# 42 gathered tokens and three products a chunk in a decoder layer's expert mixer

## The chip, the core and the metric

The kernel runs on one core of a Trainium2 chip. Its time is the device time of one launch in microseconds. The kernel before takes 2087.37 us (median of 3 runs, 2080.51 to 2088.08).

## What is computed

One layer over 264 tokens: 256 of a new sequence and 8 samples that continue sequences with a paged cache of 1024 keys and values. Cut to what matters:

```
proj = x @ w_in                                   # 2048 -> rec_x, rec_g, q, k, v (1024 each)
rec  = rg_lru(causal_conv(rec_x)) * gelu(rec_g)   # recurrence over the tokens
att  = rms_norm(diff_attention(rope(q), rope(k), v))   # samples attend to the paged cache
x1   = layer_norm(alpha * x + concat(rec, att) @ w_out)
# expert retrieval: 8 heads, product keys, the best 16 of 128 x 128 experts for a head
e, g = top_16(x1 @ wq, sub_keys), softmax(scores)
out  = sum over k of g * gelu(x1 . u[e_k]) * v[e_k]
y    = layer_norm(alpha * x1 + out)
```

All data is float32, and the tables u and v hold 16384 experts of 2048 numbers each.

## The kernel before

Activations lie with the model's dimension on the 128 partitions, in 16 chunks, and the tokens in the columns. A float32 product is made of fp32r products: each operand is split into a rounded high part (ScalarE, line 97) and a rest (VectorE, line 100), and hi x hi, hi x lo and lo x hi are summed in PSUM. Weights come in halves of 512 KB ("raw", six buffers) on SP's queue.

The program is written in one order for all engines, without a scheduler: what stands first in the code stands first on its engine. In the mixer, generators are advanced one turn at a time between groups of 12 projection products, so a `yield` more or less moves an instruction against the other engines'. The projection `proj` (lines 294 to 296) uses three products of 264 columns for each chunk. `softmax` turns the scores of the 8 samples on the cached keys into weights (`z`, `en`, matrix `C` and the products of line 596), and `values` then multiplies cached value pages. Constants are loaded on ScalarE's queue (`cload`, line 73), results of the mixer are stored on SP's.

The expert mixer treats ND = 232 of the tokens by going through all 128 blocks of 128 experts: `up` (lines 1183 and 1184) makes x1 . u for a block, `act_sum` and `act_gelu` add two halves and apply GeLU, `gate_mult` and `gate_low` multiply by the tokens' gates and split again, `down` (lines 1234 and 1235) multiplies by v, and `add` (line 1242) adds into the residual. `up` and `down` make two products for a chunk: the high weights times the high and the low activations side by side (464 columns), and the low weights times the high activations (232 columns). The two halves of the sum are put together by VectorE. Six of the up blocks are native float32 products. The other NG = 32 tokens get their experts by indirect DMA (`gathered`): 128 rows at a time, 32 tokens by 4 experts, for each table in two halves, and VectorE multiplies them (lines 1386 and 1400); turns of this generator are given out at GRATE a step of the loop. `Norm` is the layer norm, whose sums of squares run on VectorE, ScalarE and GpSimd while the last blocks are multiplied.

Of the kernel before, what the change touches and what calls it, by code (L numbers as in the profile page):

```python
# [18 lines left out]
NC_ = 16  # L19
# [4 lines left out]
NG = 32  # L24
ND = T - NG
REP = 128 // NG
RAWB = 6
# [6 lines left out]
RECB = 4  # L34
# [14 lines left out]
GRATE = 1.5  # L49
# [7 lines left out]
def _build(tc, I, O):  # L57
# [3 lines left out]
    with ctx:  # L61
# [78 lines left out]
        parts0 = pool_in(ctx, "parts0", 2, "right")  # L140
# [9 lines left out]
        own_slots = 2 * [lambda: [parts0.tile([128, 8, 128], F32R, name=k) for k in ("hi", "lo")]]  # L150
# [27 lines left out]
        ident = cload("ident", [128, 128])  # L178
        iota = cload("iota", [128, 128])
# [5 lines left out]
        cosT = cload("cosT", [128, T], pool=sa)  # L185
        sinT = cload("sinT", [128, T], pool=sa)
        blk4 = cload("blk4", [128, 4], pool=sa)
        pti = sa.tile([1, 64], I32, name="pti")
        nc.scalar.dma_start(pti, I["pt"])
        lv = sw.tile([128, 4, 64], F32, name="t", bufs=RECB)  # L190
        nc.scalar.dma_start(lv, bcast(I["lamv"], 128))
        maskn = cload("maskn", [128, 128], pool=sa)
        two = cload("two", [128, 2], pool=sa)
        cp = cload("cp", [128, 128], pool=sa)
        cn = cload("cn", [128, 128], pool=sa)
        own = cload("own", [128, 16], pool=sa)
        subg = cload("subg", [128, 1], pool=sa)
        cw = cload("cw", [128, 8, 4], pool=sa)
        cb = cload("cb", [128, 8], pool=sa)
        ba = cload("ba", [128, 8], pool=sa)  # L200
        bx = cload("bx", [128, 8], pool=sa)
        lam = cload("lam", [128, 8], pool=sa)
        h0 = cload("h0", [128, 8, 8], pool=sa)
        XS = sa.tile([128, 8, 4, 8], F32, name="XS")
        nc.scalar.dma_start(XS[:, :, 0:3, :], I["sconv"])
# [47 lines left out]
        vnat = x0w[:, 2080:2080 + 2048].rearrange("p (k d) -> p k d", k=2)  # L253
# [44 lines left out]
        def qk(g, pa, pb):  # L298
# [23 lines left out]
            else:  # L322
                nc.sync.dma_start(O["kT"][2 * (g - 4)], A)
                nc.sync.dma_start(O["kT"][2 * (g - 4) + 1], B)
# [20 lines left out]
        def vproj(h, pv):  # L345
# [5 lines left out]
            nc.sync.dma_start(O["vT"][h], vT)  # L351
# [12 lines left out]
        def head(hp, qt, h4):  # L364
# [36 lines left out]
            wT = sw.tile([128, 256], F32, name="wT", bufs=3)  # L401
# [64 lines left out]
        def rec(n, px):  # L466
# [4 lines left out]
            nc.sync.dma_start(wg, I["wax"][:, n])  # L471
# [14 lines left out]
            nc.sync.dma_start(O["convp"][:, n], last)  # L486
# [24 lines left out]
            hs = sw.tile([128, T], F32, name="hs")  # L511
# [8 lines left out]
            nc.sync.dma_start(O["hT"][:, n], hs[:, SEQ - 1:T])  # L520
# [40 lines left out]
        def softmax(sps):  # L561


            P = sx[0].tile([128, 2, 512], F32, name="cv", bufs=PAGEB)
            mx = sa.tile([128, 4], F32, name="mx")
            yield
            for a in range(2):
                nc.vector.tensor_reduce(mx[:, a:a + 1], sps[a].rearrange("p j k -> p (j k)"), op=OP.max, axis=AX.X)
            while not all(("qk", g) in done for g in range(8)):
                yield  # L570
# [11 lines left out]
            done.add("scores")  # L582
# [6 lines left out]
            nc.vector.tensor_copy(en, zz[:, 2:3].to_broadcast([128, 2]))  # L589
            yield  # L590
            W = sa.tile([128, NPG, 128], F32, name="Wk")
            for a in range(0, NPG, 4):
                yield from take("misc")
                p = pmisc([128, 4, 128])
                for j in range(4):
                    nc.tensor.matmul(p[:, j, :], P[:, a // 4, j * 128:(j + 1) * 128], C, start=True, stop=True)
                yield
                nc.scalar.copy(W[:, a:a + 4], p)
                give("misc")
# [9 lines left out]
        def values():  # L609
            while "scores" not in done:  # L610
                yield
# [41 lines left out]
            yield from rms(at, 128, 1, sw.tile([128, 1, 128], F32, name="hs"))  # L653
# [65 lines left out]
        nc.gpsimd.memset(QS, 0.0)  # L719
# [7 lines left out]
        for i, j in enumerate(seq):  # L727
# [5 lines left out]
            if i == 17:  # L733
                slots[:] = own_slots
# [25 lines left out]
        nc.sync.dma_start(O["convs"], XS[:, :, 1:4, :])  # L760
# [46 lines left out]
        class Norm:  # L807
# [43 lines left out]
            def squares(self, c):  # L851

                for k in {9: (0, 1, 2), 10: (3, 4, 8), 11: (5, 9), 12: (6, 10), 13: (7, 11, 12), 14: (13, 14), 15: (15,)}.get(c, ()):
                    self.square(k)

            def stats(self, n):

                self.totals()
                mean, rstd = self.mean, self.rstd
                nc.scalar.copy(mean, self.ps)  # L860
                nc.vector.tensor_tensor(rstd, self.ps, self.near, op=OP.subtract)
# [15 lines left out]
            def scale(self, a, n):  # L877
# [38 lines left out]
        x1s = big.tile([128, NC_, 2, T], F32R, name="A")  # L916
# [21 lines left out]
        Es = dram.tile([2, 64, 16], F32, name="Es")  # L938
# [122 lines left out]
        for m in range(2, 16):  # L1061
# [9 lines left out]
            if m < 10:  # L1071

                for c in range(2 * (m - 2), 2 * (m - 2) + 2):
                    nc.scalar.copy(x1s[:, c, 0], x1[:, c, :])
                    nc.vector.tensor_tensor(x1s[:, c, 1], x1[:, c, :], x1s[:, c, 0], op=OP.subtract)
            elif m < 14:
                rows_out(m - 10)
# [10 lines left out]
        def tokens(tt):  # L1088
# [19 lines left out]
            for bk, (a0, n) in enumerate(blocks):  # L1108
# [3 lines left out]
                for t4 in range(0, n, 4):  # L1112
                    t0 = a0 % 128 + t4
                    b = tw[0].tile([128, 4, 128], F32, name="gb", bufs=4)
                    if t4 % 8 == 0:
                        for q in range(4):
                            nc.scalar.activation(b[:, q, :], iota, AF.Abs, bias=tr[3][:, t0 + q:t0 + q + 1])
                        nc.scalar.activation(b, b, AF.Relu, scale=-1.0, bias=1.0)
                    else:
                        nc.vector.tensor_tensor(b, iota[:, None, :].to_broadcast([128, 4, 128]),  # L1120
                                                tr[1][:, t0:t0 + 4, None].to_broadcast([128, 4, 128]), op=OP.is_equal)
                    a = tw[0].tile([128, 4, 128], F32, name="ga", bufs=4)
                    for q in range(4):
# [5 lines left out]
                    def product(a=a, b=b, st=st, t4=t4, n=n, bk=bk):  # L1129
                        p = psum.tile([128, 4, 128], F32, name="acc2")  # L1130
                        for q in range(4):
                            nc.tensor.matmul(p[:, q, :], b[:, q, :], a[:, q, :], start=True, stop=True)  # L1132
                        nc.scalar.copy(st[:, :, t4:t4 + 4], p.rearrange("p t i -> p i t"))
                        if t4 + 4 == n:
# [5 lines left out]
        def gates():  # L1140
# [17 lines left out]
            nc.gpsimd.dma_start(Es[0], ef)  # L1158
            nc.gpsimd.dma_start(Es[1], top.g[:, 0])
# [12 lines left out]
        def up(k, a=0, b=NC_):  # L1172
            w = ups[k]
            if a == 0:
                pu[k] = pmm([128, 2, ND])
            p = pu[k]
            if k < NAT:
                for c in range(a, b):
                    native(p[:, 0], w, c, ND)
                return  # L1180
# [5 lines left out]
        def act_sum(k):  # L1186
            p = pu.pop(k)
            acts[k] = ex.tile([128, ND], F32, name="ac", bufs=RUN - 8)
# [358 lines left out]
```

## Time and profile before

| what | value |
|---|---|
| median of 3 runs | 2087.37 us |
| the profiled execution's own time | 2081.43 us |
| its span | 2079.7 us |
| PE busy | 1996.2 us (96%) |
| DVE busy | 1584.6 us (76%) |
| ACT busy | 973.8 us (47%) |
| POOL busy | 213.6 us (10%) |
| mean granted TensorE clock | 0.988 |
| read from HBM | 499.65 MB |

PE is TensorE's matmuls, PEld its weight loads, which run beside matmuls, DVE VectorE, ACT ScalarE, POOL GpSimd and SP the engine whose queue issues most transfers. The mixer lasts to about 470 us, its norm and the choice of experts to about 825 us, and the loop over the expert blocks to about 2050 us. A wait is shown as idle time of an engine and the instruction that ended it.

### The profile page before, as it was taken

Reading aid. Unit: us, or ns where it says so; the run is one execution under the profiler, and the core shown is the slowest. Engines: PE = TensorE matmul, PEld = TensorE weight load, DVE = VectorE, ACT = ScalarE, POOL = GpSimd, SP = SyncE. Lnnn points to the kernel's source line nnn. Section 1 sums busy time; section 2 is a strip of 40 time slices with the busy share of each in tenths; the row PEclk is TensorE's granted clock in tenths of the full one; section 3 lists DMA queues with packets and bytes.
Section 4 is the critical chain, followed back from the end, with each engine's and each line's share of the span. In section 5 each row is a group of like instructions: output and inputs, shape, how many; then the busy total and the mean of one; then the engine's idle time right before and its main releaser. Section 6 shows DMA issues by size and latency. Waiting matters only on the chain.

```text
span 2079.7 us, 37180 instructions
## 1 busy us (share of the span) xinstructions
PE 1996.2 (96%) x13890; PEld 1829.5 (88%) x13890; DVE 1584.6 (76%) x3231; ACT 973.8 (47%) x1609; POOL 213.6 (10%) x179
## 2 busy tenths in 40 slices
PE   7999789989899999999999999999999999999995
PEld 6888677789788999999999999999999999999994
DVE  5534655775599789668888888888888888878886
ACT  4223554633211798554444444444444444444444
POOL 0000000004000000001111111111222222100011
PEclk9999999999999999999999999999999999999998
DMA  8799489765344567778888888888888888866661
GB/s 283 270 364 326 154 291 318 249 204 166 105 143 135 172 235 253 259 259 292 292 287 304 280 296 300 279 286 275 289 295 277 300 302 280 302 216 219 225 208 51
DMA packets 183622, 522.07 MB, mean 251 GB/s; under 512 B 28858, under 2 KB 61650, under 8 KB 181394
## 3 DMA queue, kind: packets, MB, share of 16 engines
q1 hardware_dynamic: 160400, 451.34, 63.6%
q0 software_dynamic: 18688, 67.41, 9.7%
q8 instruction: 109, 1.79, 0.3%
q10 hardware_dynamic: 4354, 0.96, 0.2%
q14 instruction: 71, 0.58, 0.1%
HBM read 499.65 MB, written 19.97 MB: 250 GB/s over the span
## 4 chain that ended last, share of the span: by engine, by line
PE 77%; DVE 4%; ACT 3%; DMA 2%; issue 1%; POOL 1%; SPq 0%; POOLq 0%; ACTq 0%; DVEq 0%
PE mm L1183 19%; PE acc L1234 18%; PE mm L1184 9%; PE acc L1235 9%; PE mm L920 7%; PE mm L1234 3%; PE mm L1235 1%; PE acc L1132 1%; PE mm L294 1%; PE acc L635 1%; DMA cv<-in_cv 1%; PE mm L295 1%; PE mm L296 1%; DMA raw<-in_uT 1%; ACT hi L97 1%
## 5 line engine op out<-in xcount | busy, mean ns | idle before, releaser
L100 DVE TENSOR_TENSOR lo<-raw,hi 128x1024 fp32r<-128x1024 f32 x326 | 397.4, 1225 | 282.8 <-ACT hi L97 268.9
L1183 PE MATMUL mm<-A,hi 128*128 128x464 f32 x1728 | 568.3, 380 | 0.0
L1234 PE MATMUL acc<-w,xl 128*128 128x464 f32 x1640 | 532.7, 376 | 0.0
L1184 PE MATMUL mm<-A,lo 128*128 128x232 f32 x1728 | 465.8, 270 | 0.7 <-DVE lo L100 0.7
L1235 PE MATMUL acc<-w,xl 128*128 128x232 f32 x1640 | 443.0, 270 | 0.0
L97 ACT CAST hi<-raw 128x1024 fp32r<-128x1024 f32 x326 | 329.4, 1045 | 159.5 <-PE mm L295 70.3
L97 ACT CAST xl<-raw 128x1024 fp32r<-128x1024 f32 x260 | 269.2, 1046 | 220.9 <-issue 193.4
L1183 PEld LDWEIGHTS mm<-A,hi 128*128 128x128 f32 x1728 | 324.6, 188 | 42.1
L100 DVE TENSOR_TENSOR xl<-raw,xl 128x1024 fp32r<-128x1024 f32 x260 | 316.6, 1226 | 31.2 <-ACT xl L97 28.8
L1234 PEld LDWEIGHTS acc<-w,xl 128*128 128x128 f32 x1640 | 307.8, 188 | 35.9
L1184 PEld LDWEIGHTS mm<-A,lo 128*128 128x128 f32 x1728 | 330.6, 191 | 1.0 <-DVE lo L100 1.0
L1235 PEld LDWEIGHTS acc<-w,xl 128*128 128x128 f32 x1640 | 312.7, 191 | 0.0
L1217 ACT CAST w<-ac 128x232 fp32r<-128x232 f32 x128 | 49.5, 387 | 335.4 <-DVE ac L1215 332.6
L1242 DVE TENSOR_TENSOR M<-M,acc 128x232 f32<-128x232 f32 x444 | 166.9, 393 | 29.9 <-PE acc L1235 22.3
L920 PE MATMUL mm<-M,raw 128*128 128x264 f32 (+1 forms) x704 | 156.5, 383 | 7.1 <-ACT M L881 7.1
L920 PEld LDWEIGHTS mm<-M,raw 128*128 128x128 f32 x704 | 134.6, 193 | 25.6 <-ACT M L881 7.5
L294 PE MATMUL mm<-xh,hi 128*128 128x264 f32 x448 | 137.7, 307 | 14.2 <-ACT hi L97 8.3
L296 PE MATMUL mm<-xh,lo 128*128 128x264 f32 x448 | 129.5, 289 | 0.5 <-DVE lo L100 0.5
L295 PE MATMUL mm<-xl,hi 128*128 128x264 f32 x448 | 129.3, 289 | 0.2 <-DVE xl L173 0.2
L1368 POOL DMA_INDIRECT ug<-in_v,eix x64 | 87.8, 1373 | 375.5 <-DVE xrep L1400 305.3
L1368 POOL DMA_INDIRECT ug<-in_u,eix x64 | 79.6, 1244 | 441.0 <-DVE ug L1386 348.5
L294 PEld LDWEIGHTS mm<-xh,hi 128*128 128x128 f32 x448 | 86.6, 193 | 31.2 <-issue 15.5
(357 smaller groups left out, 3114.0 us busy)
## 6 DMA issues: line engine op xcount, KB each, us to landing
raw<-in_uT SPq DMA_DIRECT2D x256, 512.0 KB
raw<-in_vt SPq DMA_DIRECT2D x256, 512.0 KB
raw<-in_w_in SPq DMA_DIRECT2D x74, 512.0 KB
cv<-in_ck SPq DMA_DIRECT2D x64, 512.0 KB
cv<-in_cv SPq DMA_DIRECT2D x64, 512.0 KB
raw<-in_wq SPq DMA_DIRECT2D x32, 512.0 KB
Gd<-stage SPq DMA_DIRECT2D x14, 1024.0 KB
gt<-Gd SPq DMA_DIRECT2D x224, 64.0 KB
```

The lines of the kernel that those rows point to most:

```text
L97: nc.scalar.copy(hi, raw)
L100: (eng or nc.vector).tensor_tensor(lo, raw, hi, op=OP.subtract)
L294: nc.tensor.matmul(p, hi, xh[:, c], start=c == 0, stop=False)
L295: nc.tensor.matmul(p, hi, xl[:, c], start=False, stop=False)
L296: nc.tensor.matmul(p, lo, xh[:, c], start=False, stop=c == NC_ - 1)
L920: nc.tensor.matmul(p, w[c // 8][:, c % 8, :], x1[:, c, :n], start=c == 0, stop=c == NC_ - 1)
L1183: nc.tensor.matmul(p, hi[:, c % 8, :], x1s[:, c, :, :ND], start=c == 0, stop=False)
L1184: nc.tensor.matmul(p[:, 0, :], lo[:, c % 8, :], x1s[:, c, 0, :ND], start=False, stop=c == NC_ - 1)
L1234: nc.tensor.matmul(p[:, :, :ND], hi[:, b % 8, :], w, start=i == 0, stop=False)
L1235: nc.tensor.matmul(p[:, 0, :ND], lo[:, b % 8, :], w[:, 0], start=False, stop=i == 7)
L1242: nc.vector.tensor_tensor(a, a, p[:, b, :ND], op=OP.add)
L1368: nc.gpsimd.indirect_dma_start(out=t, out_offset=None, in_=tab, in_offset=bass.IndirectOffsetOnAxis(ap=eix[:, a, j:j + 1], axis=0))
```

## The change

NG goes from 32 to 42, so the loop treats 222 tokens and the gathers 42: the 128 gathered rows are now 42 tokens by 3 experts, and 43 turns of two halves are needed for each table in place of 32. `up` and `down` make three products of 222 columns into the same columns of PSUM; the halves' sum goes away, and `add` becomes one instruction. Some buffers change (RECB 4 to 3, three own places for split weights in place of two). Constants and the mixer's stores move to GpSimd's queue. In `softmax` a turn is taken out ahead of the exponentials and one is added behind `z`; the first value pages are asked for as soon as the keys are done. `Norm` starts its squares one column earlier, and the last scalings are shared by two engines.

```
-NG = 32
+NG = 42
+NJ = -(-128 // REP)
-RECB = 4
+RECB = 3
-GRATE = 1.5
+GRATE = 1.7
...
-        def cload(name, shape, dt=F32, pool=const):
+        def cload(name, shape, dt=F32, pool=const, eng=None):
-            nc.scalar.dma_start(t, I[name])
+            (eng or nc.scalar).dma_start(t, I[name])
...
-        parts0 = pool_in(ctx, "parts0", 2, "right")
+        parts0 = pool_in(ctx, "parts0", 3, "right")
...
-        cosT = cload("cosT", [128, T], pool=sa)
+        cosT = cload("cosT", [128, T], pool=sa, eng=nc.gpsimd)
...
-                nc.sync.dma_start(O["kT"][2 * (g - 4)], A)
+                nc.gpsimd.dma_start(O["kT"][2 * (g - 4)], A)
...
-            nc.sync.dma_start(wg, I["wax"][:, n])
+            nc.gpsimd.dma_start(wg, I["wax"][:, n])
...
             P = sx[0].tile([128, 2, 512], F32, name="cv", bufs=PAGEB)
+            done.add("P")
+            while not all(("qk", g) in done for g in range(8)):
+                yield
+            yield
             mx = sa.tile([128, 4], F32, name="mx")
-            yield
             for a in range(2):
                 nc.vector.tensor_reduce(mx[:, a:a + 1], sps[a].rearrange("p j k -> p (j k)"), op=OP.max, axis=AX.X)
-            while not all(("qk", g) in done for g in range(8)):
-                yield
...
-            C = x0w[:, :128]
-            nc.vector.scalar_tensor_tensor(C, cn, nlam, cp, op0=OP.mult, op1=OP.add)
-            yield
             zz = sa.tile([128, 4], F32, name="zz")
...
-            yield
+            yield from lag(2)
             W = sa.tile([128, NPG, 128], F32, name="Wk")
...
-            while "scores" not in done:
+            while "P" not in done:
...
-                for k in {9: (0, 1, 2), 10: (3, 4, 8), 11: (5, 9), 12: (6, 10), 13: (7, 11, 12), 14: (13, 14), 15: (15,)}.get(c, ()):
+                for k in {8: (0, 1, 2), 9: (3, 4), 10: (5, 8, 9), 11: (6, 10), 12: (7, 11), 13: (12, 13), 14: (14,), 15: (15,)}.get(c, ()):
...
+                    if both and c % 2:
+                        nc.vector.tensor_scalar(y, y, self.g[:, c:c + 1], self.b[:, c:c + 1], op0=OP.mult, op1=OP.add)
+                        continue
...
-            for c in range(a, b):
-                hi, lo = w[c // 8]
-                nc.tensor.matmul(p, hi[:, c % 8, :], x1s[:, c, :, :ND], start=c == 0, stop=False)
-                nc.tensor.matmul(p[:, 0, :], lo[:, c % 8, :], x1s[:, c, 0, :ND], start=False, stop=c == NC_ - 1)
+            else:
+                for c in range(a, b):
+                    mmc(p, w, x1s, c)
...
-                    nc.tensor.matmul(p[:, :, :ND], hi[:, b % 8, :], w, start=i == 0, stop=False)
-                    nc.tensor.matmul(p[:, 0, :ND], lo[:, b % 8, :], w[:, 0], start=False, stop=i == 7)
+                    nc.tensor.matmul(p[:, c], hi, w[:, 0], start=i == 0, stop=False)
+                    nc.tensor.matmul(p[:, c], hi, w[:, 1], start=False, stop=False)
+                    nc.tensor.matmul(p[:, c], lo, w[:, 0], start=False, stop=i == 7)
...
-            for c, p in enumerate(pv.pop(k)):
-                a = x1[:, 2 * (k % 8) + c, :ND]
-                for b in range(2):
-                    nc.vector.tensor_tensor(a, a, p[:, b, :ND], op=OP.add)
+            a = x1[:, 2 * (k % 8):2 * (k % 8) + 2, :ND]
+            nc.vector.tensor_tensor(a, a, pv.pop(k), op=OP.add)
...
-            todo = [(j, a) for j in range(NG) for a in range(2)]
+            todo = [(j, a) for j in range(NJ) for a in range(2)]
```

On TensorE, where the last chunks of an up block (`mm` from the split activations `A`) meet the first of a down block (`acc` from the weighted activations `w`), before:

```order
L1183 MATMUL mm<-A,hi 128x464
L1184 MATMUL mm<-A,lo 128x232
L1234 MATMUL acc_13788<-w,xl 128x2x232
L1235 MATMUL acc_13788<-w,xl 128x232
L1234 MATMUL acc_13788<-w,xl 128x2x232
```

And the same place in the changed kernel:

```order
L106 MATMUL mm<-A,hi 128x222
L107 MATMUL mm<-A,hi 128x222
L108 MATMUL mm<-A,lo 128x222
L1228 MATMUL acc_14972<-w,hi 128x222
L1229 MATMUL acc_14972<-w,hi 128x222
L1230 MATMUL acc_14972<-w,lo 128x222
```

Two products a chunk became three, and the third is as long as the others.

On VectorE, in the mixer, the sum `z` of the sample rows' softmax behind an attention head (`sc`, `st`), before:

```order
L394 SCALAR_TENSOR_TENSOR sc<-sc,st 128x256
L510 TENSOR_TENSOR i<-i,t 128x264
L512 SCALAR_TENSOR_TENSOR hs<-r,i 128x256
L513 TENSOR_TENSOR hs<-r,c_h_192 128x8
L514 TENSOR_TENSOR hs<-hs,i 128x8
L518 TENSOR_TENSOR gg<-gg,hs 128x264
L476 TENSOR_SCALAR cv<-mm,c_cw,c_cb 128x256
L478 SCALAR_TENSOR_TENSOR cv<-mm,c_cw,cv 128x253
...
L384 TENSOR_SCALAR st<-st 128x2
L275 TENSOR_TENSOR A<-sq,A 128x4x128
L585 TENSOR_REDUCE z<-zz 128x1
```

And in the changed kernel:

```order
L396 TENSOR_SCALAR sc<-sc,st 128x256
L397 SCALAR_TENSOR_TENSOR sc<-sc,st 128x256
L587 TENSOR_REDUCE z<-zz 128x1
L588 RECIPROCAL z<-z 128x1
L589 TENSOR_SCALAR M<-M,z 128x128
L591 COPY en<-zz 128x2
L513 TENSOR_TENSOR i<-i,t 128x264
```

The sum and what follows from it moved ahead of a recurrence (`hs`, `gg`), a convolution (`cv`) and a weight split.

On ScalarE, the exponentials of the same softmax (`cv,zz<-acc`), before:

```order
L387 ACTIVATE sc,st<-sc,st 128x256 x2
L508 ACT_TABLE_LOAD
L508 ACTIVATE t<-t 128x264
L463 ACT_TABLE_LOAD
L463 ACTIVATE gg<-gg 128x264
L273 CAST A<-sq 128x4x128
L579 ACT_TABLE_LOAD
L579 ACTIVATE cv,zz<-acc_835,mx 128x512
```

And in the changed kernel:

```order
L390 ACTIVATE sc,st<-sc,st 128x256 x2
L580 ACTIVATE cv,zz<-acc_838,mx 128x512
L580 ACTIVATE cv,zz<-acc_839,mx 128x512
L582 ACTIVATE zz<-sn,mx 128x1
L511 ACT_TABLE_LOAD
L511 ACTIVATE t<-t 128x264
```

The exponentials now stand ahead of the square root and the GeLU, behind the head's exponentials, whose function they share.

## Rows read from the trace of the kernel before

**Rows 1.** Busy time of each engine, from the page: us, share, instructions.

```profile
PE 1996.2 (96%) x13890; PEld 1829.5 (88%) x13890; DVE 1584.6 (76%) x3231; ACT 973.8 (47%) x1609; POOL 213.6 (10%) x179
```

**Rows 2.** Sums by stretch: length, PE PEld DVE ACT POOL busy, clock, DMA, GB/s.

```profile
0.00:52.00 52.00, 37.18 (x271) 36.36 (x272) 28.19 (x46) 22.74 (x30) 2.26 (x6) 0.93 0.84 283
208.00:260.00 52.00, 41.10 (x348) 35.80 (x336) 34.79 (x85) 30.62 (x66) 0.00 (x0) 0.93 0.47 154
1508.00:1560.00 52.00, 52.00 (x324) 48.31 (x324) 44.65 (x69) 24.66 (x36) 11.51 (x8) 1.00 0.87 295
1872.00:1924.00 52.00, 52.00 (x326) 48.42 (x325) 44.81 (x92) 23.48 (x32) 0.00 (x0) 1.00 0.65 219
```

**Rows 3.** Timeline of PE in the expert loop: start, length, line, tiles, shape.

```profile
1203.26 0.38 PE L1234 MATMUL acc<-w,xl 128*128 128x464 f32 x1
1208.39 0.38 PE L1183 MATMUL mm<-A,hi 128*128 128x464 f32 x1
1208.60 0.27 PE L1184 MATMUL mm<-A,lo 128*128 128x232 f32 x1
1213.57 0.38 PE L1234 MATMUL acc<-w,xl 128*128 128x464 f32 x1
```

**Rows 4.** Timeline of weight loads and products that add the gathered tokens.

```profile
1848.83 3.65 PEld L1405 LDWEIGHTS misc<-c_selM,xrep 128*128 128x128 f32 x32
1848.93 3.66 PE L1405 MATMUL misc<-c_selM,xrep 128*128 128x32 f32 x32
```

**Rows 5.** Timeline of weight loads in the expert loop.

```profile
1200.23 0.19 PEld L1183 LDWEIGHTS mm<-A,hi 128*128 128x128 f32 x1
1200.34 0.19 PEld L1184 LDWEIGHTS mm<-A,lo 128*128 128x128 f32 x1
1200.56 0.19 PEld L1183 LDWEIGHTS mm<-A,hi 128*128 128x128 f32 x1
```

**Rows 6.** Timeline of PE in the mixer's projection.

```profile
99.74 0.28 PE L295 MATMUL mm<-xl,A 128*128 128x264 f32 x1
101.19 0.28 PE L295 MATMUL mm<-xl,A 128*128 128x264 f32 x1
```

**Rows 7.** Groups by line, residual adds: count, busy us, mean ns, idle before.

```profile
L1242 DVE TENSOR_TENSOR M<-M,acc 128x232 f32<-128x232 f32 x444 | 166.9, 393 | 29.9 <-PE acc L1235 22.3
```

**Rows 8.** Waits of PE: line, releaser, us in total, times, longest.

```profile
PE mm L294 <- ACT hi L97: 8.3, 1, 8.3
PE misc L596 <- DVE en L589: 8.1, 1, 8.1
PE acc L555 <- DMA cv<-in_ck: 7.5, 12, 0.9
PE acc L635 <- DMA cv<-in_cv: 7.2, 4, 2.7
PE misc L830 <- POOL ug L828: 5.4, 2, 4.0
```

**Rows 9.** Timelines of DVE, ACT and PE around the fourth weight tile.

```profile
27.01 0.43 DVE L310 TENSOR_TENSOR QB<-r,i 128x264 f32<-128x264 f32 x1
33.34 1.99 ACT L97 CAST hi<-raw 128x1024 fp32r<-128x1024 f32 x2 [13.68 <-DMA c_lam<-in_lam]
34.44 0.59 PE L294 MATMUL mm<-xh,hi 128*128 128x264 f32 x1 [8.28 <-ACT hi L97]
```

**Rows 10.** Timelines of DVE and ACT around the sample rows' softmax.

```profile
235.66 0.48 DVE L394 SCALAR_TENSOR_TENSOR sc<-sc,st 128x256 f32<-128x256 f32 x1
245.46 0.15 DVE L585 TENSOR_REDUCE z<-zz 128x1 f32<-128x3 f32 x1
237.69 0.69 ACT L579 ACTIVATE cv<-acc,mx 128x512 f32<-128x512 f32 x1
```

**Rows 11.** Timelines of PE and ACT at the end.

```profile
2055.22 1.94 PE L830 MATMUL misc<-ug,ones 128*128 128x264 f32 x4 [4.00 <-POOL ug L828]
2068.37 8.08 ACT L881 ACTIVATE M<-M,c_ln2b,c_ln2g 128x264 f32<-128x264 f32 x16 [5.21 <-DVE M L872]
```

More of the change, by code (lines that the diff above doesn't have):

```diff
@@ L149, in _build @@
         room = mixes[0].rearrange("p c s t -> p (c s t)")
-        own_slots = 2 * [lambda: [parts0.tile([128, 8, 128], F32R, name=k) for k in ("hi", "lo")]]
+        own_slots = 3 * [lambda: [parts0.tile([128, 8, 128], F32R, name=k) for k in ("hi", "lo")]]
         slots.extend(own_slots + [lambda k=k: place(room, k) for k in range(4)])
@@ L400, in head @@
             yield
[L401 removed]
+            wT = sw.tile([128, 256], F32, name="wT", bufs=2)
             nc.scalar.copy(wT[:, :nk], pw)
@@ L485, in rec @@
             yield
-            nc.sync.dma_start(O["convp"][:, n], last)
+            nc.gpsimd.dma_start(O["convp"][:, n], last)
             yield from lag(RLAG)
@@ L581, in softmax @@
             nc.scalar.activation(zz[:, 2:3], sn, AF.Exp, bias=mx[:, 3:4])
-            done.add("scores")
+            C = x0w[:, :128]
+            nc.vector.scalar_tensor_tensor(C, cn, nlam, cp, op0=OP.mult, op1=OP.add)
             yield
@@ L589, in softmax @@
             nc.vector.tensor_copy(en, zz[:, 2:3].to_broadcast([128, 2]))
-            yield
[L591 to L596, printed above, removed]
-                yield
-                nc.scalar.copy(W[:, a:a + 4], p)
-                give("misc")
+            yield from lag(2)
+            W = sa.tile([128, NPG, 128], F32, name="Wk")
+            yield from take("misc", 2)
+            ps = [pmisc([128, 4, 128]) for _ in range(2)]
+            for j in range(NPG):
+                nc.tensor.matmul(ps[j // 4][:, j % 4, :], P[:, j // 4, j % 4 * 128:(j % 4 + 1) * 128], C, start=True, stop=True)
+            yield
+            for a in range(2):
+                nc.scalar.copy(W[:, 4 * a:4 * a + 4], ps[a])
+            give("misc", 2)
             Wk.append(W)
@@ L652, in values @@
             at = acc[:, None, :]
-            yield from rms(at, 128, 1, sw.tile([128, 1, 128], F32, name="hs"))
+            yield from rms(at, 128, 1, sw.tile([128, 1, 128], F32, name="hs", bufs=1))
             yield from take("misc")
@@ L1127, in tokens, with product @@
                         prev.pop(0)()
-                    def product(a=a, b=b, st=st, t4=t4, n=n, bk=bk):
+                    def product(a=a, b=b, st=st, t4=t4, w=w, n=n, bk=bk):
                         p = psum.tile([128, 4, 128], F32, name="acc2")
-                        for q in range(4):
+                        for q in range(w):
                             nc.tensor.matmul(p[:, q, :], b[:, q, :], a[:, q, :], start=True, stop=True)
-                        nc.scalar.copy(st[:, :, t4:t4 + 4], p.rearrange("p t i -> p i t"))
-                        if t4 + 4 == n:
+                        nc.scalar.copy(st[:, :, t4:t4 + w], p[:, :w].rearrange("p t i -> p i t"))
+                        if t4 + w == n:
                             nc.sync.dma_start(Gd[bk], st)
@@ L1402, in gathered @@
             yield from ahead(I["v2"], acc)
-            pf = pmisc([128, NC_, NG])
-            for c in range(NC_):
-                nc.tensor.matmul(pf[:, c, :], accg[:, c * 128:(c + 1) * 128], selM, start=True, stop=True)
-            nc.vector.tensor_tensor(x1[:, :, ND:], x1[:, :, ND:], pf, op=OP.add)
+            for h in (0, 8):
+                pf = pmisc([128, 8, NG])
+                for c in range(8):
+                    nc.tensor.matmul(pf[:, c, :], accg[:, (h + c) * 128:(h + c + 1) * 128], selM, start=True, stop=True)
+                nc.vector.tensor_tensor(x1[:, h:h + 8, ND:], x1[:, h:h + 8, ND:], pf, op=OP.add)
         gg = gathered()
```

145 lines of the change are left out of this document (66 added, 79 removed).

## The prediction

> **What bounds the kernel now.** I read the page's busy times first, then the sums by stretch, then the waits of PE, and last the timelines of PE and of its weight loads where the change edits the products. The page shows PE busy for 96% of the span, DVE for 76% and ACT for 47% [rows 1]. The stretches show where the missing 4% lies: in the expert loop PE is busy 52.00 of 52.00 us (1508 to 1560, DVE 44.65, ACT 24.66, DMA 0.87), while the start (37.18) and the stretch 208 to 260 (41.10) have holes, both with a mean granted clock of 0.93 [rows 2]; the end has another [rows 11]. So two accounts must be kept apart: a product of the expert loop costs its own time in full, and outside it an edit is worth the hole that it closes. The reader is to see in the timeline that one expert's up block takes 5.18 us (1208.39 to 1213.57) and a down block 5.13 us (1203.26 to 1208.39), back to back, with no wait written behind a row [rows 3]. Each has 16 pairs of a 464-column and a 232-column product: 0.324 and 0.321 us a pair. There are 122 up blocks (128 less the 6 native ones) and 128 down blocks: 250 x 5.15 us, 62% of the span.
>
> **The expert products, on the path.** A pair (696 columns, two weight loads) becomes three products of 222 columns (666 columns, three weight loads). By columns alone that is 4% less. But each product has its own load of 128 x 128 weights, and the loads have a pace of their own. The row to look at is the run of 32 loads at 1848.83: 3.65 us in all, each 0.19 long, so 31 steps in 3.46 us: 0.1115 us from load to load [rows 4]. The products that they serve have only 32 columns, so it is not the columns that set this pace. In the pairs a load that starts with the short product is followed by the next after 0.11 us (1200.23 to 1200.34), as long as the 232-column product takes in the pair, and the next one only at 1200.56, when the 464-column product ends [rows 5]: one load of the two lies under a product twice as long as itself. With three short products no load has such a cover. What 222 columns need by themselves I take from the mixer, where three products into the same columns run already: 12 of 264 columns from 99.74 to 101.19, 0.1208 us each [rows 6], or 0.1016 for 222. That is less than 0.1115, so the load sets the pace: a block takes 48 x 0.1115 = 5.35 us. Up: 122 x (5.35 - 5.18) = +20.7 us; down: 128 x (5.35 - 5.13) = +28.2 us; together +49. There are 12,000 such products, so each nanosecond of the pace is 12 us, and the pace at which nothing changes is a third of a pair, 0.107 to 0.108. The ends are +49 (loads as at 1848) and, if loads are hidden, 48 x 0.1016 = 4.88 us a block: 122 x -0.30 and 128 x -0.25, or -69. I take the first end, since the row is of loads that follow each other without a pause, which is what the change makes.
>
> The Trainium skill (TensorE: Matmul & The Clock Gate, "LDWEIGHTS (loading the stationary operand)") gives a load of P columns P/1.2 ns, 106.7 for 128. By that figure, an estimate, a block would take 5.12 us and the term would be -9 in place of +49; the run at 1848 measures 0.1115, and I go by it.
>
> **What the products no longer cost elsewhere.** DVE loses the sum of two halves per expert and four adds into the residual for one of 444 columns; the adds are 0.393 us each [rows 7]. ACT loses a copy. All this lay beside PE, which is busy 52.00 of 52, and counts nothing; it pays for the extra gathers. Those are 86 in place of 64 for each table, and 1.7 in place of 1.5 turns a step. A step's DVE work was 44.65/52 of 10.31, 8.9 us; it loses about 2.0 less 0.8 for the wide add, and gains 0.2 turns of some 1.3 us: 8 of 10.7 us, with room. DMA: the loop alone has 0.65, with gathers 0.87 [rows 2]; 1.7/1.5 of the difference over a longer step leaves it at 0.87. The 181 turns end at step 107 of 128, before the forced drain at 118. Cost nothing; if PE ran at 4.88 a block the DMA share would be 0.95, and a late tile would then show.
>
> **The start.** PE waits 8.3 us once for the split of the fourth weight tile [rows 8]. ACT is idle for 13.68 us before that split, in which it issues the constants' transfers; the row names one of them as what ended the idle time [rows 9]. They go to POOL, which has nothing to do then. ACT can split once the first tiles are done; next late is DVE's rotation of the first query pair, which frees the product bank and ends at 27.44 [rows 9]. PE went on at 34.44 after 8.28 us of waiting, so it had stopped at 26.2; some 7 of the 8.3 us can go, and part of the 7% that the clock lost in the first stretch. But 104 to 208 is fed by transfers, and PE there waits 7.5 us for key pages in 12 pieces [rows 8], which come no sooner. I take -6, from 0 to -10.
>
> **The softmax of the sample rows.** PE waits 8.1 us for `en` [rows 8]. On DVE the last steps of an attention head end at 236.1, but the sum `z` stands behind a whole recurrence and convolution and runs at 245.46, though ACT's exponentials, behind two table loads, had begun by 237.7 [rows 10]. In the changed order `z` stands right behind that head and the exponentials ahead of the two other tables; the products stand at the same place in PE's order. All inputs are then there by about 238, where PE stopped. I take -9: 8.1, and 1 for the clock, which fell to 1.2 GHz for a while after such a stop (0.93 in that stretch). From -3 to -11.
>
> **Stores off SP, pages earlier.** Weight and page loads no longer stand behind stores on SP; three value pages are asked for before the scores are done. PE waits 7.2 us for value pages in 4 pieces [rows 8]. I take -3, from -10 to +10: the other sign is POOL's queue, where a recurrence's gate weights now stand behind stores that wait for earlier results, and RECB 3 in place of 4.
>
> **Norms, end, small things.** Squares begin one column earlier and PE's last hole of 4.0 us, which waits for POOL's chain of sums, closes; ACT's 16 last scalings (8.08 us) become 14 with two on DVE, -1.0 [rows 11]. With the first norm's 1.4 of the 5.4 us for POOL [rows 8]: -6, from 0 to -9. Two gather-matrix products fewer are 16 loads at 0.1115, -1.8; ten columns of four passes in 96 native products at 2.4 GHz, -1.6.
>
> **Sum.** 2081.4 (the profiled execution; span 2079.7) + 49 - 6 - 9 - 3 - 6 - 3.4 = 2103 us, 1.0% more. The median of the three runs is 2087.4, 0.3% over the profiled one, which is the spread of one kernel.
>
> **Rivals.**
> A. *Break-even loads.* A load in this data type takes 0.107 to 0.108, not 0.1115. For it: in the pairs load to load is 0.11 at two decimals and the 232-column product leaves no more than about 0.107 [rows 3, 5]. Against it: there the load before it had been done long ago. The loop then stays, and the other terms leave 2081 - 27 = 2054. By the page's 106.7 it would be 2045.
> B. *Loads hidden, columns count.* -69 and -27: 1985 us. For it: the three-product form at 264 columns runs at its columns' pace [rows 6]. Against it: 264 columns take longer than a load; no row here has products with loads of their own closer than 0.10.
> C. *The mixer gives nothing back.* POOL's in-order queue delays gate weights in 8 recurrences by some 2 us each, and the two holes close only half: 2103 + 15 = 2118.
>
> **Chances.** My forecast 0.58, with a range of its own of 2088 to 2117 from the terms outside the loop; A 0.20; B 0.14; C 0.08. The range reaches from 2046 to 2122 and leaves out B and a little at the edges. About 0.5% is what a measurement of this kernel can tell from no change. Slower by more: three quarters of the forecast, C, and a tenth of A, 0.52. Faster: nearly all of A, B and a little of the forecast, 0.33. Within: 0.15.
>
> **What would show it.** Right: in the expert loop, weight loads every 0.111 to 0.112 us and blocks of 5.35 us, PE still at 52 of 52, DVE lower than before; the hole before the fourth weight tile under 2 us, and none before the softmax's products. Wrong: blocks of 5.15 us or less, which is A, or 4.9 us, which is B; products at 1.00 clock that start closer than 0.107; or waits of PE for `wg` or the cosines.

## The result and the profile after

The changed kernel takes 2099.46 us (median of 5 runs, 2095.88 to 2104.59), the kernel before 2083.96 (5 runs, 2080.51 to 2088.08): ratio 1.0076, 95% interval 1.0053 to 1.0099. It is 0.8% slower. The forecast was 2103, in a range from 2046 to 2122. The profiled execution took 2104.59 us with a span of 2102.8.

The first row of the page, busy time by engine, answers to [rows 1]:

```profile
PE 2038.6 (97%) x17870; PEld 1966.6 (94%) x17870; DVE 1487.3 (71%) x2783; ACT 932.2 (44%) x1478; POOL 360.5 (17%) x301
```

PE is busy for 42 us more than before, and the weight loads for 137 us more; DVE has 97 us less. Nearly 4,000 products and as many loads came in. The same by stretch (columns as in [rows 2]; a fifth row is added for the stretch that follows the fourth):

```profile
0.00:52.00 52.00, 43.52 (x332) 42.36 (x333) 32.87 (x62) 24.64 (x34) 13.48 (x26) 1.00 0.86 303
208.00:260.00 52.00, 46.30 (x381) 39.41 (x379) 37.36 (x89) 29.85 (x66) 3.24 (x6) 0.93 0.57 185
1508.00:1560.00 52.00, 52.00 (x468) 52.00 (x467) 39.15 (x48) 22.10 (x29) 15.38 (x9) 1.00 0.89 304
1872.00:1924.00 52.00, 51.16 (x455) 50.74 (x454) 43.62 (x61) 18.96 (x26) 15.33 (x13) 1.00 0.90 317
1924.00:1976.00 52.00, 48.10 (x417) 47.01 (x416) 45.02 (x67) 20.01 (x27) 10.76 (x8) 1.00 0.84 289
```

Three things are to be seen. The start and the softmax's stretch have 6.3 and 5.2 us more of PE's work in the same 52 us. In the middle of the expert loop PE still has no hole, but now PEld has none either: 52.00 of 52.00. And at 1872 to 1976, where PE had been full before ([rows 2] and the row below), it has holes of 0.84 and 3.90 us, which the prediction did not see.

```profile
1924.00:1976.00 52.00, 52.00 (x326) 48.42 (x325) 44.70 (x91) 23.67 (x31) 0.00 (x0) 1.00 0.67 225
```

PE's products in one up block and at the start of the next down block (timeline: start, us, engine, line, operation):

```profile
1507.98 0.28 PE L106 MATMUL mm<-A,xl 128*128 128x222 f32 x1
1508.09 0.27 PE L107 MATMUL mm<-A,xl 128*128 128x222 f32 x1
1508.20 0.27 PE L108 MATMUL mm<-A,xl 128*128 128x222 f32 x1
1508.31 0.28 PE L106 MATMUL mm<-A,xl 128*128 128x222 f32 x1
...
1513.34 0.27 PE L1228 MATMUL acc<-w,hi 128*128 128x222 f32 x1
```

The up block begins with the first of these rows, so it takes 1513.34 - 1507.98 = 5.36 us for 48 products, 0.1117 each. Its weight loads, from the timeline of PEld:

```profile
1508.21 0.19 PEld L106 LDWEIGHTS mm<-A,xl 128*128 128x128 f32 x1
1508.32 0.19 PEld L107 LDWEIGHTS mm<-A,xl 128*128 128x128 f32 x1
1508.43 0.19 PEld L108 LDWEIGHTS mm<-A,xl 128*128 128x128 f32 x1
```

Every load, whichever of the three products it serves, follows the last by 0.11 us. In [rows 5] every second one came 0.22 us after the one ahead.

What PE waits for now (waits by line: total, times, longest), against [rows 8]:

```profile
PE acc L637 <- DMA cv<-in_cv: 3.1, 4, 1.2
PE misc L597 <- ACT wT L405: 2.8, 1, 2.8
PE misc L605 <- ACT Wk L600: 2.6, 1, 2.6
PE acc L1230 <- DVE xl L101: 1.6, 2, 0.8
```

Of the 8.3 us for the fourth weight tile's split a hole of 1.4 us is left, in which PE waits for DVE's half of a split (its row stands with the constants' run below); the value pages cost 3.1 us in place of 7.2. The softmax's 8.1 us became two waits of 2.8 and 2.6, and the last row is one of three of the same size at L1230, which are new.

### The profile page after: what moved, and what is told of

It reads as the page before. It is cut to its first block, busy times and chain, and to the rows that moved or that the text cites. A ratio compares the mean times of both kernels' runs of the same rounds, so it can differ in the third digit from the quotient of the medians.

```text
span 2102.8 us, 44520 instructions
## 1 busy us (share of the span) xinstructions
PE 2038.6 (97%) x17870; PEld 1966.6 (94%) x17870; DVE 1487.3 (71%) x2783; ACT 932.2 (44%) x1478; POOL 360.5 (17%) x301
## 4 chain that ended last, share of the span: by engine, by line
PE 80%; DVE 8%; DMA 6%; ACT 3%; issue 2%; SPq 1%; POOL 0%; POOLq 0%; ACTq 0%; DVEq 0%
PE mm L108 10%; PE mm L107 10%; PE mm L106 10%; PE acc L1230 9%; PE acc L1228 9%; PE acc L1229 9%; PE mm L925 7%; PE mm L297 2%; DMA cv<-in_ck 2%; PE mm L298 2%; PE mm L299 2%; DVE lo L101 2%; DMA cv<-in_cv 2%; PE acc L1137 1%; DMA raw<-in_uT 1%
## 5 line engine op out<-in xcount | busy, mean ns | idle before, releaser
L108 PE MATMUL mm<-A,lo 128*128 128x222 f32 (+1 forms) x1256 | 346.0, 275 | 2.7 <-DVE lo L101 2.7
L106 PE MATMUL mm<-A,hi 128*128 128x222 f32 (+1 forms) x1256 | 347.8, 277 | 0.0
L107 PE MATMUL mm<-A,hi 128*128 128x222 f32 (+1 forms) x1256 | 346.2, 276 | 0.0
L1230 PE MATMUL acc<-w,lo 128*128 128x222 f32 x1048 | 286.5, 273 | 1.6 <-DVE lo L101 1.6
L1228 PE MATMUL acc<-w,hi 128*128 128x222 f32 x1048 | 288.0, 275 | 0.0
L1229 PE MATMUL acc<-w,hi 128*128 128x222 f32 x1048 | 287.5, 274 | 0.0
L108 PEld LDWEIGHTS mm<-A,lo 128*128 128x128 f32 x1256 | 241.2, 192 | 3.1 <-DVE lo L101 3.1
L107 PEld LDWEIGHTS mm<-A,hi 128*128 128x128 f32 x1256 | 241.2, 192 | 0.1
L106 PEld LDWEIGHTS mm<-A,hi 128*128 128x128 f32 x1256 | 241.1, 192 | 0.1
L106 PE MATMUL mm<-A,xl 128*128 128x222 f32 (+1 forms) x824 | 229.0, 278 | 0.0
L108 PE MATMUL mm<-A,xl 128*128 128x222 f32 (+1 forms) x824 | 226.8, 275 | 0.4 <-DVE xl L101 0.4
L107 PE MATMUL mm<-A,xl 128*128 128x222 f32 (+1 forms) x824 | 226.8, 275 | 0.0
L1230 PEld LDWEIGHTS acc<-w,lo 128*128 128x128 f32 x1048 | 201.2, 192 | 1.9 <-DVE lo L101 1.9
L1228 PEld LDWEIGHTS acc<-w,hi 128*128 128x128 f32 x1048 | 201.2, 192 | 0.1
L1229 PEld LDWEIGHTS acc<-w,hi 128*128 128x128 f32 x1048 | 201.2, 192 | 0.0
L1230 PE MATMUL acc<-w,xl 128*128 128x222 f32 x728 | 199.4, 274 | 1.6 <-DVE xl L101 1.6
```

The costliest lines, as they stand in the source:

```text
L106: nc.tensor.matmul(p, hi[:, c % 8, :], x[:, c, 0], start=c == first, stop=False)
L107: nc.tensor.matmul(p, hi[:, c % 8, :], x[:, c, 1], start=False, stop=False)
L108: nc.tensor.matmul(p, lo[:, c % 8, :], x[:, c, 0], start=False, stop=c == last)
L1228: nc.tensor.matmul(p[:, c], hi, w[:, 0], start=i == 0, stop=False)
L1229: nc.tensor.matmul(p[:, c], hi, w[:, 1], start=False, stop=False)
L1230: nc.tensor.matmul(p[:, c], lo, w[:, 0], start=False, stop=i == 7)
```

## The experiments

Each ran beside runs of the kernel before on its own chip, and ratios are to those. The changed kernel's own is 1.0076.

**The loop's products alone.** The kernel before, with NG still 32, and only `up`, `down` and `add` (with the activation's call) as in the changed kernel:

```
-                nc.tensor.matmul(p, hi[:, c % 8, :], x1s[:, c, :, :ND], ...)
-                nc.tensor.matmul(p[:, 0, :], lo[:, c % 8, :], x1s[:, c, 0, :ND], ...)
+                    mmc(p, w, x1n, c)        # x1n: the ND columns of x1s
```

> The kernel before with 32 gathered tokens and nothing changed but the expert products: three of 232 columns into the same columns. Load theory: 232 columns need 0.106 us, still less than a load, so weight loads come every 0.111 to 0.112 us, blocks take 5.36 us, the step 10.7 us, and the time is 2084 + 48 = 2132, ratio 1.023. Column theory: the pace grows with the columns, 0.1115 x 232/222 = 0.1165, blocks 5.59, about 2189, ratio 1.05. If the cause lies in the other parts of the change: 2084, ratio 1.00.

Measured: 2128.23 us against 2081.26, ratio 1.0221 (1.0199 to 1.0243), +47 us. The first product of an up block, of the next down block and of the next up block, from PE's timeline:

```profile
1499.52 0.28 PE L105 MATMUL mm<-A,hi 128*128 128x232 f32 x1
...
1504.88 0.28 PE L1224 MATMUL acc<-w,xl 128*128 128x232 f32 x1
...
1510.24 0.28 PE L105 MATMUL mm<-A,hi 128*128 128x232 f32 x1
```

Both blocks take 5.36 us, as with 222 columns. The loads' theory holds and the columns' theory (5.59) falls; the loop's whole loss comes from the form of the products.

**Fewer moving columns.** The changed kernel with 128 columns in 23 of a down chain's 24 products; most of columns 128 to 221 of the down result is left out:

```
+                    n = ND if i == 0 else 128
-                    nc.tensor.matmul(p[:, c], hi, w[:, 0], ...)
+                    nc.tensor.matmul(p[:, c, :n], hi, w[:, 0, :n], ...)      # the other two: :128
```

> The changed kernel with 128 in place of 222 moving columns in all but one of the 24 products of a down chain, at full weight loads; most of the down result of columns 128 to 221 is left out. Load theory: the pace is the load's, whatever the columns, so weight loads still come every 0.111 to 0.112 us, a down block takes 5.36 us, and the time stays at 2099. Column theory: 46 of 48 products fall with their columns, to 0.065 us or less, a block to 3.2 us, 128 x -2.1 = -270, or as far as DVE and the transfers let it. Between: 222 columns and the load both count for a little, and the loads fall to 0.107 or 0.108; block 5.15 to 5.2, about 2075.

Measured: 2223.18 us (2 runs), ratio 1.0679 (1.0649 to 1.0709): slower, though its loop has a fifth fewer columns to stream. PE's timeline in a down block:

```profile
1199.76 0.28 PE L1230 MATMUL acc<-w,hi 128*128 128x128 f32 x1
1199.87 0.28 PE L1231 MATMUL acc<-w,lo 128*128 128x128 f32 x1
1199.98 0.28 PE L1229 MATMUL acc<-w,hi 128*128 128x128 f32 x1
1200.10 0.27 PE L1230 MATMUL acc<-w,hi 128*128 128x128 f32 x1
```

The pace is 0.111 with 128 columns as with 222, and up and down together took 10.72 us a step until the up blocks ended, to 0.01 us the step of the changed kernel. So 42% fewer columns in a product buy nothing. The loss came after the last up block, where only these down blocks are left (windows, columns as above; the last three figures are the granted clock, the DMA share and GB/s):

```profile
1860.00:1900.00 40.00, 40.00 (x361) 40.00 (x360) 32.94 (x45) 14.38 (x20) 11.75 (x8) 1.00 0.88 300
...
1960.00:2020.00 60.00, 60.00 (x283) 60.00 (x282) 23.95 (x38) 11.75 (x15) 0.00 (x0) 0.50 0.33 104
```

The granted clock falls to 0.50, 1.2 GHz, while PE is written as busy for all 60 us: 283 products in 60 us, 0.212 each. No theory had that. PE's timeline shows the moment: 39 us after the last up block's end comes the stretch's only wait, and 1.6 us after that wait the pace goes from 0.111 to 0.212.

```profile
1910.80 0.33 PE L1231 MATMUL acc<-w,lo 128*128 128x128 f32 x1 [0.82 <-DVE lo L101]
...
1912.31 0.29 PE L1229 MATMUL acc<-w,hi 128*128 128x128 f32 x1
...
1912.82 0.41 PE L1229 MATMUL acc<-w,hi 128*128 128x128 f32 x1
1913.03 0.41 PE L1230 MATMUL acc<-w,hi 128*128 128x128 f32 x1
```

In the changed kernel, with 222 columns, the same stretch keeps 1.00, and six waits of 0.78 us in it do not bring the clock down. Whether the narrow products alone or the wait on top of them did it here, no run separates.

**Shorter weight loads.** The changed kernel with 64 of 128 weight columns in 22 of 24 products of a down chain, at 222 moving columns; half of the down result's columns are left out:

```
+                    n, m = 128 if i == 0 else 64, 128 if i == 7 else 64
-                    nc.tensor.matmul(p[:, c], hi, w[:, 0], ...)
+                    nc.tensor.matmul(p[:n, c], hi[:, :n], w[:, 0], ...)     # then :64, and :m for lo
```

> The changed kernel with 64 in place of 128 columns of weights in 22 of every 24 products of a down block, at the same 222 moving columns; half of the down result's columns are left out. Load theory, if a load's time goes with its weight columns: these products fall to their columns' pace, 0.1016 us, so a down block takes 4.9 us, 128 x -0.44 = -57, about 2043, while the up blocks stay at 5.36. If a load of 64 columns takes as long as one of 128, or if the moving columns set the pace: both blocks 5.36, about 2099.

Measured: 2059.70 us, ratio 0.9891 (0.9867 to 0.9915), 40 us less than the changed kernel. From PE's timeline, a down block and the first product behind it:

```profile
1507.78 0.27 PE L1229 MATMUL acc<-w,xl 128*128 128x222 f32 x1
1507.89 0.27 PE L1230 MATMUL acc<-w,xl 128*64 128x222 f32 x1
1508.00 0.26 PE L1231 MATMUL acc<-w,xl 128*64 128x222 f32 x1
1508.10 0.26 PE L1229 MATMUL acc<-w,xl 128*64 128x222 f32 x1
...
1512.79 0.28 PE L106 MATMUL mm<-A,hi 128*128 128x222 f32 x1
```

The block falls to 5.01 us; with four full loads at 0.111 the other 44 products take (5.01 - 0.45)/44 = 0.104 us each. Both suspects have now been cut by themselves: cutting the columns does nothing, cutting the load gives time back. The shorter loads also leave half of the result's rows unwritten, but the run with 128 columns wrote 42% less and gained nothing, so that is not the reason. The size was off: 0.104, not the 0.1016 scaled from 264 columns. At 0.104 a block of 48 would take 4.97 us where the prediction's rival B took 4.88; whether the 222 columns or the load of 64 sets the 0.104, no run separates.

**All the rest alone.** The changed kernel with the earlier pair of products, NG 32, 1.5 turns a step and, for room, three gather buffers in place of four:

```
-NG = 42
+NG = 32
...                                  # up, act_sum, act_gelu, down, add as before
```

> The changed kernel with the earlier pair of products, 32 gathered tokens and 1.5 gather turns a step (three instead of four gather buffers, for room): only the mixer's and the norms' parts of the change are left. Forecast of the prediction for these parts: -6 -9 -3 -6 -1 = -25 or so, and since the queries' first product came 25 us earlier in the changed kernel and its end was shorter, 2050 to 2060, ratio 0.985. Rival (the mixer's parts give nothing back by themselves): 2078 to 2084, ratio 0.997 to 1.00.

Measured: 2042.80 us, ratio 0.9805 (0.9784 to 0.9827), -38 us where 25 were forecast. Some of the surplus is in the loop: an up block takes 5.14 us (median of the loop's) against 5.195 before, and 122 x 0.055 = 6.7 us. In `up` only the layout of the split activations differs: `x1s` was 264 columns wide with 232 used, and is now as wide as it is used, so that the 464 columns lie side by side. The down blocks, whose operand had no gap before either, take 5.14 and 5.15 us. No run changed the layout alone.

**Parts taken back, one by one**, in the changed kernel: the constants on ACT's queue, the softmax's order with the value pages' request, the stores and gate weights on SP, and the norms' squares and scalings:

```
-        cosT = cload("cosT", [128, T], pool=sa, eng=nc.gpsimd)            # and 19 more
+        cosT = cload("cosT", [128, T], pool=sa)
...
-                for k in {8: (0, 1, 2), 9: (3, 4), 10: (5, 8, 9), ...
+                for k in {9: (0, 1, 2), 10: (3, 4, 8), 11: (5, 9), ...
```

> The changed kernel with the constants' transfers back on ACT's queue. The prediction gave 6 us to their move: PE again waits about 8 us for the split of the fourth weight tile, the first 52 us show PE at 37 of 52 instead of 43.5, and the time is 2099.5 + 6 = 2105. Rival (the gain of the start is lost again before the queries, to the key pages): 2099 with the hole back.

Measured: 2110.96 us, ratio 1.0133 (1.0109 to 1.0157). The hole is back, PE has 37.84 of the first 52 us, and the first native float32 product, which follows the mixer and its norm, comes at 513.57 instead of 506.00. The rows are from the waits of this run, from its timeline of PE, and from PE's timeline of the changed kernel:

```profile
PE mm L297 <- ACT A L98: 7.8, 1, 7.8
```

```profile
513.57 0.81 PE L925 MATMUL mm<-M,raw 128*128 128x264 f32 x1 [6.75 <-ACT M L886]
```

```profile
29.48 0.39 PE L299 MATMUL mm<-xh,A 128*128 128x264 f32 x1 [1.37 <-DVE A L101]
...
506.00 0.81 PE L925 MATMUL mm<-M,raw 128*128 128x264 f32 x1 [6.75 <-ACT M L886]
```

The moment of that product is not steady. In the eight profiled executions with the mixer as changed (the changed kernel and the seven runs here that change only what follows it) it lies between 496.8 and 506.0, so the trace puts the constants at 7.6 to 16.8 us. The two ratios put them at 12 us, give or take 7; 6 were forecast.

> The changed kernel with the sample rows' softmax in the order of before (the sum behind two yields, the products in two halves, value pages asked for after the scores). The prediction gave 9 us to the new order: PE waits about 8 us for the sums again in the stretch 208 to 260, and the time is 2108. Rival (the hole only moves, since other heads fill it): 2099 to 2102.

Measured: 2102.34 us, ratio 1.0096 (1.0072 to 1.0120), not told apart from the changed kernel; the first native product comes at 502.1, within the spread just named. The hole is back (first row, waits of this run), but in the changed kernel the same products wait as well (rows of PE's timeline there, and of DVE's for the sum):

```profile
PE misc L599 <- DVE en L592: 6.7, 1, 6.7
```

```profile
224.34 0.16 DVE L587 TENSOR_REDUCE z<-zz 128x1 f32<-128x3 f32 x1 [0.38 <-ACT zz L582]
...
230.26 1.16 PE L597 MATMUL misc<-M,cv 128*128 128x128 f32 x8 [2.77 <-ACT wT L405]
237.85 0.38 PE L605 MATMUL misc<-en,M 128*128 128x2 f32 x1 [2.61 <-ACT Wk L600]
```

The sum is ready at 224.5, and the products begin 5.8 us later: they now take two banks of `misc` at once, and one of them is free only when ACT has copied an attention head's transposed weights (`wT`). That copy ends at 230.2; ACT had stood for 3.2 us until 222.67, where the exponentials at the head of its order got their maxima from DVE, and had worked without a pause since. The row vector's product then waits for ACT's copies of both halves. What DVE gave, ACT's copies took: 8.1 us became 2.8 and 2.6. The value pages, asked for late again in this run, cost PE 3.0 us against 3.1, so the early request shows no gain either.

> The changed kernel with the mixer's stores and the gate weights' loads back on SP's queue; value pages are still asked for early. The prediction gave 3 us (from -10 to +10) to stores and pages together: 2102, with PE's waits for value pages back to 5 to 7 us from 3.1. Rival (SP's queue was not what the pages waited for): 2099, waits as in the changed kernel.

Measured: 2104.96 us, ratio 1.0105 (1.0076 to 1.0135). The waits for value pages are 4.2 us against 3.1, but in the other runs that leave this part as changed they are anything from 0.7 to 4.4, and the first native product comes at 505.9, within the spread. So the trace shows no price; the two ratios give 6 us, give or take 8.

> The changed kernel with the norms' squares begun one column later, as before, and all last scalings on ACT. The prediction gave these 6 us less a little: 2104, with the last hole before POOL's sums back at 4 us from 1.2 and the hole of the first norm a little longer. Rival (the tail has other work of the same length): 2099 to 2101.

Measured: 2103.63 us, ratio 1.0110 (1.0076 to 1.0144). PE's two waits for POOL's sums are 3.8 us against 2.7, and the tail behind the last down product's end is 26.0 us against 24.2. So 2 us by the trace; the two ratios give 7 us, give or take 9.

**The gathers in the last steps.** The changed kernel with a higher rate:

```
-GRATE = 1.7
+GRATE = 1.95
```

> The changed kernel with 1.95 in place of 1.7 gather turns a step. The prediction costed the extra gathers at nothing. Theory: they do cost, at one place: 181 turns at 1.7 end at step 107, while from step 94 on a step has only a down block (5.4 us) and DVE cannot do a step's work and 1.7 turns in it, so PE waits about 0.8 us for a split six times between 1916 and 1961. At 1.95 they end at step 93; these waits go, and the time falls by 4 to 7, to about 2094. Rival (the transfers are the limit; their share of 0.86 in the loop rises to 0.9 and a weight tile comes late): 2099 or more.

Measured: 2094.73 us, ratio 1.0056 (1.0038 to 1.0074), 5 us less; the two intervals overlap, so only the trace can tell. The stretches that had the holes:

```profile
1872.00:1924.00 52.00, 52.00 (x468) 52.00 (x467) 31.57 (x54) 20.15 (x28) 0.00 (x0) 1.00 0.63 210
1924.00:1976.00 52.00, 52.00 (x468) 52.00 (x467) 34.56 (x58) 22.22 (x29) 0.00 (x0) 1.00 0.64 216
```

PE is full again, all six waits of 0.78 us are gone, and the last gathered row is added at 1870 instead of 1961. The six waits are 4.7 us.

**42 tokens with the pair of products.** The changed kernel with `up`, `down` and `add` in the earlier form, at 444 and 222 columns:

> The changed kernel with 42 gathered tokens and all its other parts, but with the expert products in the earlier form: a 444-column and a 222-column product per weight tile. Load theory (in the three-product form each product waits for its own weight load, 0.1115 us): a pair again has one load under the long product, so a pair takes about 0.207 + 0.11 = 0.317 us, a block 5.05 us against 5.36; 250 blocks give -77, about 2022 us, ratio to the kernel before 0.97. Column theory (222 columns in this form simply take 0.1115): 666 columns cost the same, blocks 5.36, about 2099, ratio 1.007. Third theory (a shorter step leaves DVE or the transfers late, since the gathers now take 1.7 turns a step): blocks near 5.05 but PE waits in the loop, 2040 to 2070.

Measured: 2060.85 us, ratio 0.9895 (0.9870 to 0.9919): the third theory. Up blocks took 5.01 us, but with the gathers the down blocks waited, and the steps, from 10.0 to 10.8 us long, took 10.3 to 10.4 on average in place of 10.02. DVE's timeline in such a step, and ACT's:

```profile
1509.40 0.17 DVE L1221 TENSOR_TENSOR ac<-ac,gt 128x14 f32<-128x14 f32 x1
1510.96 1.23 DVE L101 TENSOR_TENSOR lo<-raw,hi 128x1024 fp32r<-128x1024 f32 x1 [1.39 <-ACT hi L98]
```

```profile
1509.61 0.38 ACT L1223 CAST w<-ac 128x222 fp32r<-128x222 f32 x1 [2.74 <-DVE ac L1221]
1509.89 1.99 ACT L98 CAST hi<-raw 128x1024 fp32r<-128x1024 f32 x2
```

ACT stands for 2.74 us at a copy that needs DVE's gate product; its weight split is queued behind, and then DVE stands for 1.39 us for that split. Each waits for the other once a step. So the copy goes behind the split, and the subtraction behind the split's second half:

```
             split1(d, n, 0)
             if k >= 0:
-                gate_low(k)
+                gate_high(k)            # the copy, taken out of gate_mult
             split1(d, n, 1)
+            if k >= 0:
+                gate_low(k)
```

> The run with the pair form and 42 tokens, with one step's order changed: ACT copies the gated activations only after its next weight split, and DVE subtracts their low half after the second half of that split. Theory: the shorter step of 10.03 us lost 0.3 us because DVE waited 1.39 us a step for a split on ACT that stood behind a copy that waited for DVE; with that wait gone the blocks stay at 5.01 through the gathers, 97 x -0.3 = -30, about 2031, ratio 0.976. Rival: DVE has too much work in 10 us with 1.7 gather turns a step; the step stays at 10.3 to 10.4 and the time at 2055 to 2061.

Measured: 2028.89 us, ratio 0.9745 (0.9725 to 0.9765), as forecast. DVE's wait is 0.26 us and both blocks take 5.01. The two moves were not tried apart. What was left are the last steps, and with 1.95 turns a step:

> The pair form with 42 tokens and the reordered step (2029 us), with 1.95 turns a step as well. There PE waits 10 us in the last steps, between 1823 and 1888, for splits on DVE behind gathers; with the gathers ended before, 2029 - 10 = 2019, ratio 0.970. Rival: in steps of 10.03 us DVE then has 9.3 us of work and the transfers a share of 0.93; splits come late all through the loop, and the time is 2029 to 2040.

Measured: 2016.05 us, ratio 0.9682 (0.9649 to 0.9715). The stretch in the middle of the loop, and one in the last steps:

```profile
1508.00:1560.00 52.00, 52.00 (x334) 49.72 (x333) 49.07 (x74) 27.03 (x37) 15.96 (x12) 1.00 0.91 313
1800.00:1852.00 52.00, 52.00 (x333) 49.84 (x332) 39.49 (x83) 21.77 (x30) 0.00 (x0) 0.97 0.62 208
```

DVE is at 94% there and PE still has no hole. This version beats both kernels: by 3.2% the one before, and by 83 us the changed one.

## Why the prediction was right

**The products: right, in mechanism and size.** The forecast was loads at 0.1115 us, blocks of 5.35 and +49 us. The trace has 0.1117 and 5.36, and the products alone make +47. Reading the pace of the loads off 32 narrow products elsewhere in the same trace [rows 4] was what decided it. The figure of the Trainium skill (TensorE: Matmul & The Clock Gate, "LDWEIGHTS (loading the stationary operand)"), P/1.2 ns and so, as an estimate, 106.7 for 128 columns, would have made the change a gain; the runs measure 111 to 112 where loads follow each other without a pause. The sustained spacing that the Trainium skill gives in the same page's section "Back-to-back issue gap" for 128 moving columns, about 81 ns, does not hold for this kernel's products either: with 128 columns they were 111 ns apart.

**Rivals A and B fall** by blocks of 5.36 where A needed at most 5.15 and B 4.9. Rival C falls by the run with the rest alone, -38 us.

**The start: right, but too small.** -6 forecast, 7.6 or more by the trace. The hole was to be under 2 us and is 1.37.

**The softmax: wrong.** The step that failed is "All inputs are then there by about 238, where PE stopped. I take -9": it counted the operands and not the bank that the result goes to. Two holes of 5.4 us in all took the place of 8.1, and taking the order back costs nothing that can be measured.

**Stores and pages: no gain seen.** -3 was forecast. Neither the stores nor the early request, taken back, shows a price in the traces; the times would allow one.

**Norms and end: about half.** -6 was forecast. PE's last hole closes from 4.0 to 1.2 us, and the tail behind the last down product's end is 24.2 us in place of 29.4. In the run with the loop's products alone, which has the old norms, it is 27.5; so 1.9 of the 5.2 us come with the products and 3.3 with the norms. The first norm's wait of 1.4 us, counted as gone, is still 1.5.

**Gathers "cost nothing": wrong by 5 us.** The prediction reckoned DVE's room in a step of 10.7 us, and saw that the gathers end at step 107. But from step 94 a step has only its down block. By DVE's rows there two splits (2 x 1.22), the gate (0.37 + 0.17), the low half (0.39), the wide add (0.61) and 1.7 turns of 1.28 make 6.2 us against 5.4, and PE waits. Before, 1.5 turns and fewer rows ended with the up blocks (the last row at 1847, the last up block at 1863).

**The sum.** +47 for the products, -38 for the rest and +5 for the gathers make +14. The 38 us have a part that the three-product form cannot use (the 6.7 us of an up block's operand, since loads bound that form); without it the sum is +21. Measured is +15.5; each ratio is good to some 4 to 5 us, so the measurements cannot tell the two sums apart. From the mixer and its norm the trace has 25 us, the first native product at 506.0 in place of 531.2 (527.7 in the run with the loop's products alone). Ahead of that product PE is idle for 36.8 us in place of 58.1. By its waits the start gave 6.9 of these 21, key and value pages together 6.9 (14.6 to 7.8), the softmax 2.7, and the attention heads 3.6, by a wait that the prediction did not name and that is now gone:

```profile
PE misc L399 <- DVE sc L394: 3.6, 4, 1.4
```

Only the constants' share is shown by an edit. The pages' waits are 4.4 to 10.9 us from run to run with the new mixer. The wait for `sc` is absent in all of these runs, also where one of the four parts was taken back, so none of the four made that gain alone. The third place for split weights and the later switch of those places were not tried apart, nor two parts together, and so what closed these holes stays open.

The total is right in part by luck. As a difference +22 was forecast (2103 against 2081.4) and +15.5 measured; the forecast started from an execution 2.5 us below the median of before. The rest of the change gave some 10 us more than was forecast, by other ways than those named, and the gathers took 5 back. Two small readings of the prediction are off and change nothing: the gather matrices lose 20 products (464 to 444) and not 16, and its parts for a slower kernel add up to 0.535 where it has 0.52.

## What to carry to other kernels

A product whose columns stream in less time than its own weight load takes is priced by the load, here 0.111 us for 128, 222 and 232 columns alike: read the pace of back-to-back loads from narrow products in the same trace, and keep one wide product per pair so that its load is covered, even if the narrow form streams fewer columns. Before a faster step is counted as a gain, look for two in-order engines that wait for each other once a step; one copy and one subtraction, each moved behind a split, were worth 32 us here. When work beside the loop is spread by a rate, check where it ends against where the steps become short, and when a wait is removed, name the bank that the next result needs, not only the operands.

## What was not expected of the hardware

- With 128 moving columns and no up blocks between, the granted clock went to 0.50 (1.2 GHz) after a wait of 0.8 us and stayed there until near the end, though PE is shown as busy for 60.00 of 60 us; the same loads with 222 columns kept 1.00 through waits of the same length. The products were then 0.212 us apart, and 124 us were lost against the changed kernel. Here narrower products did not only fail to gain.
- The pair at 444 and 222 columns takes 5.01/16 = 0.313 us against 0.321 at 464 and 232: 2.5% less time for 4.3% fewer columns.
